# A LoRA projection bound by its DMA: first load ahead of the entry barrier, small loads on a second queue, and one chunk's casting held back until two stores have landed

## Chip, cores, metric

The kernel runs on one core of a Trainium2 chip. The metric is the device time of one execution in microseconds, lower is better. Where two kernels are compared, they ran on the same chip, in alternating rounds.

## The reference

```python
x_flat = x.reshape(-1, in_dim)             # 32768 x 256, float32
y = x_flat @ W                             # W: 256 x 256
lora_out = (x_flat @ lora_A) * lora_E      # rank 16
y = y + scale * (lora_out @ lora_B)
return y.reshape(batch, seq_len, out_dim).astype(np.float32)
```

The input x is 33.6 MB and the output is 33.6 MB. Both cross between HBM and SBUF once (the page of the kernel before: HBM read 33.85 MB, written 33.56 MB), so the kernel moves 67 MB whatever it computes.

## The kernel before

The kernel folds the LoRA part into one weight, `weff = W + A diag(E) B`, and then works on 8 chunks of 4 MB. A chunk is loaded into one of 6 "homes" in SBUF. It is treated in 8 groups: GpSimd casts a group to bf16, TensorE transposes it, ScalarE copies the transposed group out of PSUM, TensorE multiplies, and VectorE writes the result back over the input in the home. Then the home is stored. Two homes are used twice, so chunks 6 and 7 can be loaded only after chunks 0 and 1 are stored.

All DMAs are issued by SyncE (SP), in this order:

```python
ORDER = ["L0", "L1", "L2", "L3", "L4", "L5",
         "S0", "S1", "L6", "L7", "S2", "S3", "S4", "S5", "S6", "S7"]

def sync_program():
    def load(pc):
        c, s, e = pc
        if c >= N_HOMES:
            sync.wait_ge(stored_of[c - N_HOMES], 16)
        sync.dma_start(out=home(c)[:, s:e, :], in_=x_chunks[c, :, s:e, :]).then_inc(loaded[pc], 16)

    load(pieces[0])                        # first 1 MB of chunk 0
    for name, to, of in (("w", ...), ("a", ...), ("e", ...), ("b", ...)):
        sync.dma_start(out=to[:], in_=of).then_inc(set_up_loaded[name], 16)
    for step in ORDER:
        ...                                # loads as above; a store waits for its chunk:
        sync.wait_ge(s_chunk, c + 1)
        sync.dma_start(out=y_chunks[c], in_=home(c)[:]).then_inc(stored_of.get(c, stored_rest), 16)

def gpsimd_program():
    ...                                    # identity matrix for the transposes
    for g in range(N_GROUPS):              # 64 groups
        c, b = g // GPC, g % GPC * CG
        for pc in pieces:
            if pc[0] == c and pc[1] == b:
                gpsimd.wait_ge(loaded[pc], 16)
        if g >= NS:
            gpsimd.wait_ge(s_turned, g - NS + 1)
        gpsimd.tensor_copy(out=stage[g % NS][:], in_=home(c)[:, b:b + CG, :]).then_inc(s_stage, 1)
    ...

# ... (scalar_program, vector_program, tensor_program cut)
with tc.tile_critical(no_gpsimd_drain=True):
    sync_program(); gpsimd_program(); scalar_program(); vector_program(); tensor_program()

def wait_for_stores(nc):
    nc.sync.wait_ge(stored_rest, 16 * N_HOMES).then_inc(stored_rest, -16 * N_HOMES)

nc.at_finalize(wait_for_stores)
```

Of the kernel before, what the change touches and what calls it, by code (L numbers as in the profile page):

```python
# [15 lines left out]
N_HOMES = 6  # L16
# [5 lines left out]
]  # L22

EARLY_AFTER = 1

CG = 4
GPC = ROWS // CG
# [8 lines left out]
def kernel(  # L36
# [10 lines left out]
    nc = tc.nc  # L47
# [5 lines left out]
    KT = K // P  # L53
    assert N == N_CHUNKS * ROWS * P and K == M and KT == 2

    x_chunks = x_flat.rearrange("(c p b) k -> c p b k", p=P, b=ROWS)
# [8 lines left out]
    w_sb = sbuf("w_sb", [P, KT, M], FP32)  # L65
    a_sb = sbuf("a_sb", [P, KT, R], FP32)
    b_sb = sbuf("b_sb", [R, M], FP32)
    e_sb = sbuf("e_sb", [R, 1], FP32)
# [5 lines left out]
    pieces = []  # L74
    for c in range(N_CHUNKS):
        s = 0
# [3 lines left out]
    loaded = {pc: sem(f"loaded_{pc[0]}_{pc[1]}") for pc in pieces}  # L80
    set_up_loaded = {n: sem(f"loaded_{n}") for n in ("w", "a", "b", "e")}
    stored_of = {c: sem(f"stored_{c}") for c in range(N_CHUNKS - N_HOMES)}
    stored_rest = nc.alloc_semaphore("stored_rest")
# [12 lines left out]
    def home(c):  # L96
        return homes[c % N_HOMES]

    sync, gpsimd, scalar, vector, tensor = nc.sync, nc.gpsimd, nc.scalar, nc.vector, nc.tensor

    def sync_program():
        def load(pc):
            c, s, e = pc
            if c >= N_HOMES:
                sync.wait_ge(stored_of[c - N_HOMES], 16)
            sync.dma_start(out=home(c)[:, s:e, :], in_=x_chunks[c, :, s:e, :]).then_inc(loaded[pc], 16)

        load(pieces[0])
        for name, to, of in (
            ("w", w_sb, W.rearrange("(q t) m -> q t m", t=KT)),  # L110
            ("a", a_sb, lora_A.rearrange("(q t) r -> q t r", t=KT)),
            ("e", e_sb, lora_E[:, None]),
            ("b", b_sb, lora_B),
        ):
            sync.dma_start(out=to[:], in_=of).then_inc(set_up_loaded[name], 16)
        for step in ORDER:
            c = int(step[1:])
            if step[0] == "L":
                for pc in pieces:
                    if pc[0] == c and pc != pieces[0]:  # L120
                        load(pc)
                if c == EARLY_AFTER:

                    sync.wait_ge(s_first, 1)
                    sync.dma_start(out=y_chunks[0, :16, 0, :32], in_=home(0)[:16, 0, :32]).then_inc(s_early, 16)
            else:
                sync.wait_ge(s_chunk, c + 1)
                if c == 0:
                    sync.wait_ge(s_early, 16)
                sync.dma_start(out=y_chunks[c], in_=home(c)[:]).then_inc(stored_of.get(c, stored_rest), 16)  # L130

    def gpsimd_program():
        gpsimd.memset(ident[:], 0.0).then_inc(s_ident, 1)  # L133
        gpsimd.wait_ge(s_ident, 1)
        gpsimd.affine_select(  # L135
            out=ident[:],
            in_=ident[:],
            compare_op=ALU.not_equal,
            fill=1.0,
            base=0,  # L140
            pattern=[[-1, P]],
            channel_multiplier=1,
        ).then_inc(s_ident, 1)
        for g in range(N_GROUPS):
            c, b = g // GPC, g % GPC * CG
            for pc in pieces:
                if pc[0] == c and pc[1] == b:
                    gpsimd.wait_ge(loaded[pc], 16)
            if g >= NS:
                gpsimd.wait_ge(s_turned, g - NS + 1)  # L150
            gpsimd.tensor_copy(out=stage[g % NS][:], in_=home(c)[:, b:b + CG, :]).then_inc(s_stage, 1)  # L151

        gpsimd.wait_ge(s_turned, N_GROUPS - NS + 1)
        gpsimd.drain().then_inc(s_stage, 1)

    def scalar_program():
        for g in range(N_GROUPS):
            scalar.wait_ge(s_turned, g + 1)
            if g >= NX:
                scalar.wait_ge(s_y, g - NX + 1)  # L160
            halves = psum_xt[g % NT][:].bitcast(BF16).rearrange("q b (p t) -> q b t p", t=KT)
            scalar.copy(out=xt[g % NX][:], in_=halves).then_inc(s_xt, 1)  # L162

    def vector_program():
        vector.wait_ge(set_up_loaded["e"], 16)
        vector.wait_ge(s_pe_set_up, 1)
        vector.tensor_scalar(  # L167
            out=ate[:],
            in0=psum_y[0][:R, :KT, :P],
            scalar1=e_sb[:],  # L170
            scalar2=float(scale),
            op0=ALU.mult,
            op1=ALU.mult,
        ).then_inc(s_ate, 1)
        vector.wait_ge(set_up_loaded["w"], 16)
        vector.wait_ge(s_pe_set_up, 2)
        vector.tensor_add(out=weff[:], in0=w_sb[:], in1=psum_y[1][:, :KT, :]).then_inc(s_free, NY)  # L177
        for g in range(N_GROUPS):
            c, b = g // GPC, g % GPC * CG
            vector.wait_ge(s_y, g + 1)  # L180
            vector.tensor_copy(out=home(c)[:, b:b + CG, :], in_=psum_y[g % NY][:]).then_inc(s_free, 1)  # L181
            if g == 0:
                vector.drain().then_inc(s_first, 1)
            if g % GPC == GPC - 1:
                vector.drain().then_inc(s_chunk, 1)

    def tensor_program():
        def take(s):
            tensor.wait_ge(s, 1).then_inc(s, -1)  # L189

        def turn(i):
            take(s_stage)

            words = stage[i % NS][:].bitcast(FP32)
            for b in range(CG):
                ins = tensor.transpose(psum_xt[i % NT][:, b, :], words[:, b, :], ident[:])  # L196
            ins.then_inc(s_turned, 1)

        def multiply(i):
            take(s_xt)  # L200
            take(s_free)
            for b in range(CG):
                for t in range(KT):
                    ins = tensor.matmul(  # L204
                        psum_y[i % NY][:, b, :],
                        xt[i % NX][:, b, t, :],
                        weff[:, t, :],
                        start=(t == 0),
                        stop=(t == KT - 1),
                    )  # L210
            ins.then_inc(s_y, 1)

        tensor.wait_ge(s_ident, 2)
        tensor.wait_ge(set_up_loaded["a"], 16)
        for t in range(KT):
            ins = tensor.transpose(psum_y[0][:R, t, :P], a_sb[:, t, :], ident[:])  # L216
        ins.then_inc(s_pe_set_up, 1)
        turn(0)
        tensor.wait_ge(set_up_loaded["b"], 16)
        tensor.wait_ge(s_ate, 1)  # L220
        for t in range(KT):
            ins = tensor.matmul(psum_y[1][:, t, :], ate[:, t, :], b_sb[:], start=True, stop=True)  # L222
        ins.then_inc(s_pe_set_up, 1)
        assert N_GROUPS % UNROLL == 0 and all(UNROLL % n == 0 for n in (NS, NX, NT, NY))
        with tensor.Fori(0, N_GROUPS // UNROLL):
            for i in range(UNROLL):
                turn(i + 1)
                multiply(i)

    with tc.tile_critical(no_gpsimd_drain=True):  # L230
        sync_program()
        gpsimd_program()
        scalar_program()
        vector_program()
        tensor_program()

    def wait_for_stores(nc):
        nc.sync.wait_ge(stored_rest, 16 * N_HOMES).then_inc(stored_rest, -16 * N_HOMES)

    nc.at_finalize(wait_for_stores)  # L240


# [33 lines left out]
```

## Time and profile before

| | before |
|---|---|
| time, median (lowest to highest) | 163.35 us (163.25 to 163.46, 3 runs) |
| profiled span | 162.0 us |
| bytes moved, mean rate over the span | 67.43 MB, 416 GB/s |
| compute ends (last VectorE copy) | 121.2 us |
| last DMA completion | 162.0 us |

The page of the kernel before. The first lines give busy time; in the part with 40 slices each digit is the busy share of one slice, about 4 us, in tenths.

```profile
span 162.0 us, 2150 instructions
PE 96.9 (60%) x778; PEld 80.1 (49%) x778; DVE 79.6 (49%) x66; ACT 66.1 (41%) x65; POOL 67.1 (41%) x70
...
PE   0399928999999999999900089999960000000000
...
DMA  5999898999999997999999999999999999999992
...
DMA packets 2979, 67.43 MB, mean 416 GB/s; under 512 B 528, under 2 KB 544, under 8 KB 672
```

No compute engine is busy for more than 60% of the span, and TensorE is done after three quarters of it. The DMA row reads 7 to 9 tenths from the second slice to the last but one. So the kernel can get faster only where DMA time is lost, and that is at its two ends and in packets that take longer than they should. Note the three empty slices in TensorE's row: between 82 and 93 us it has nothing to do although DMA is loading.

The head, by the timeline (start, duration, engine, line, what; "SPq" is the SP queue issuing a DMA):

```profile
0.94 0.38 SPq L106 DMA_DIRECT2D home<-in_x_dram  x1
...
1.38 0.42 SPq L115 DMA_DIRECT2D w_sb<-in_W_dram  x1
...
3.59 1.37 SPq L106 DMA_DIRECT2D home<-in_x_dram  x3
```

The first load is issued at 0.94 us, and its first packet starts at 1.95. The view of SP's waits says what it waited for before that (engine and line, releaser, us in total, times, longest): 0.7 us, for TensorE at the entry barrier.

```profile
SPq L257 <- PEq L257: 0.7, 1, 0.7
```

GpSimd's casts around the idle stretch, by its timeline; the bracket is the idle time before the instruction and what ended it:

```profile
76.09 1.04 POOL L151 CAST stage<-home 128x1024 bf16<-128x1024 f32 x1 [0.38 <-PE psum_xt L196]
77.48 1.04 POOL L151 CAST stage<-home 128x1024 bf16<-128x1024 f32 x1 [0.35 <-PE psum_xt L196]
92.77 2.03 POOL L151 CAST stage<-home 128x1024 bf16<-128x1024 f32 x2 [14.24 <-DMA home<-in_x_dram]
```

The sixth chunk is cast up to 78.5 us, and then nothing can be cast until chunk 6 has been loaded. During these casts, and until 83 us, DMA is storing chunks 0 and 1. During the idle stretch it is loading.

One fact is not in these views: the duration of the single DMA packets, which the trace records. Of the 1920 packets of 32 KB, 1453 take exactly 1213 ns and most others 1214 to 1221. The trace does not say which of the 16 DMA engines moved a packet, but packets that follow each other at their own distance form a chain. I listed the 32 KB packets of 1260 to 1345 ns, called "slow packets" below. In the kernel before they are, from 62 us on:

```
start of the slow packets, us
beside stores 0 and 1, compute running:  64.6 65.9 67.2 68.5 69.7 71.0 72.3 72.4 73.6 74.9 76.2 77.5 78.7 80.0
beside loads 6 and 7 (83 to 100 us):     none
beside stores 2 and 3, compute running:  100.2 104.8 106.1 107.3 108.6 109.9 111.2 112.5 113.8 115.1 116.4 117.6 118.9 121.4 122.7
```

With few exceptions (72.4, 100.2) each starts when the one before has ended (within a row of them the starts are 1.27 to 1.32 us apart), so I take them for the packets of one engine. (The one at 72.4 follows an 8 KB packet that fetched instructions, the page's "q14 instruction", at 72.05 us. It overlaps the packet before it in the list, so I give it to another engine.) That engine falls behind. Packets longer than 1345 ns are not in the list: they stand at the turns from loads to stores (near 60 and 100 us) and beside later instruction fetches, and one of 1619 ns at 100.7 us seems to be of the same engine, so not quite all of its lag comes from slow packets. The trace has 16 completions for each large load or store, which I take for one of each engine, and the kernel's waits are for all 16. For the last store the median of the 16 completions is at 159.80 us, the second-last at 160.21 and the last at 162.00. The kernel ends when this one engine does.

### The profile page before, as it was taken

The page shows a single profiled execution, that of the slowest core. Times are in us where ns is not written, and L with a number is a line of the kernel's source. Part 1 is how long each engine was busy: PE and PEld are TensorE (multiplying, and loading weights), DVE is VectorE, ACT ScalarE, POOL GpSimd, SP SyncE. Part 2 cuts the span into 40 slices and gives each one's busy share as a digit, 9 for nine tenths or more (in the row PEclk, how much of TensorE's full clock was granted, in tenths as well). Part 3 has the DMA queues.
Part 4 walks back from the last instruction along what each step waited for, and adds up shares of the span by engine and source line. Part 5 has one row for each costly group of instructions (what it writes and reads, how often), then busy time and mean ns, then how long its engine had stood idle before and what let it go on. Part 6 is the DMA issues. An engine that isn't in the chain of part 4 may idle for free. (4 is left out here: it accounts for less than half of the span.)

```text
span 162.0 us, 2150 instructions
## 1 busy us (share of the span) xinstructions
PE 96.9 (60%) x778; PEld 80.1 (49%) x778; DVE 79.6 (49%) x66; ACT 66.1 (41%) x65; POOL 67.1 (41%) x70
## 2 busy tenths in 40 slices
PE   0399928999999999999900089999960000000000
PEld 0268817888888888888800068888840000000000
DVE  0116854888888888888830017888880000000000
ACT  3044725777767677777700026676720000000000
POOL 1455518777777677777200066677500000000000
PEclk9999999999999999999995558999995555555555
DMA  5999898999999997999999999999999999999992
GB/s 166 419 455 457 388 518 388 388 518 388 388 518 388 388 512 324 461 390 429 469 396 429 469 396 429 455 421 429 445 429 429 445 421 453 421 429 445 421 429 105
DMA packets 2979, 67.43 MB, mean 416 GB/s; under 512 B 528, under 2 KB 544, under 8 KB 672
## 3 DMA queue, kind: packets, MB, share of 16 engines
q1 hardware_dynamic: 2976, 67.41, 97.5%
q14 instruction: 3, 0.02, 0.0%
HBM read 33.85 MB, written 33.56 MB: 416 GB/s over the span
## 5 line engine op out<-in xcount | busy, mean ns | idle before, releaser
L181 DVE COPY home<-psum_y 128x1024 f32<-128x1024 f32 x64 | 78.4, 1225 | 31.9 <-PE psum_y L204 29.9
L151 POOL CAST stage<-home 128x1024 bf16<-128x1024 f32 x64 | 66.4, 1042 | 47.8 <-DMA home<-in_x_dram 26.0
L162 ACT COPY xt<-psum_xt 128x1024 bf16<-128x1024 bf16 x64 | 64.8, 1012 | 51.6 <-PE psum_xt L196 51.6
L204 PE MATMUL psum_y<-weff,xt 128*128 128x256 bf16 x512 | 68.4, 278 | 0.4
L204 PEld LDWEIGHTS psum_y<-weff,xt 128*128 128x128 bf16 x512 | 47.0, 99 | 14.4 <-issue 6.4
L196 PE MATMUL psum_xt<-ident,stage 128*128 128x128 f32 x260 | 41.1, 283 | 16.0 <-PEq L189 16.0
L196 PEld LDWEIGHTS psum_xt<-ident,stage 128*128 128x128 f32 x260 | 31.9, 147 | 18.1 <-issue 17.2
L216 PE MATMUL psum_y<-ident,a_sb 128*16 128x128 f32 x2 | 0.6, 394 | 6.6 <-DMA a_sb<-in_lora_A_dram 6.6
L167 DVE TENSOR_SCALAR ate<-psum_y,e_sb 16x256 f32<-16x256 f32 x1 | 0.5, 472 | 7.3 <-PE psum_y L216 7.3
L216 PEld LDWEIGHTS psum_y<-ident,a_sb 128*16 128x16 f32 x2 | 0.1, 90 | 6.6 <-issue 6.6
L222 PE MATMUL psum_y<-b_sb,ate 16*128 16x256 f32 x4 | 2.1, 670 | 0.0
L177 DVE TENSOR_TENSOR weff<-w_sb,psum_y 128x512 bf16<-128x512 f32 x1 | 0.7, 689 | 2.4 <-PE psum_y L222 2.4
L162 ACT ACT_TABLE_LOAD x1 | 1.3, 1283 | 0.9 <-SPq L230 0.9
L222 PEld LDWEIGHTS psum_y<-b_sb,ate 16*128 16x128 f32 x4 | 1.2, 319 | 0.5 <-issue 0.3
L133 POOL MEMSET ident<- 128x128 f32 x1 | 0.2, 206 | 0.5 <-SPq L230 0.5
L135 POOL TENSOR_SCALAR_AFFINE_SELECT ident<-ident 128x128 f32<-128x128 f32 x1 | 0.3, 293 | 0.2 <-POOL ident L133 0.2
L257 POOL MEMSET const-float32-0.0<- 128x1 f32 x1 | 0.1, 99 | 0.2 <-issue 0.2
L257 POOL MEMSET const-bfloat16-1.0<- 128x1 bf16 x1 | 0.1, 103 | 0.0
L257 POOL MEMSET const-uint8-127<- 128x1 uint8 x1 | 0.1, 103 | 0.0
L257 POOL MEMSET const-float32-1.0<- 128x1 f32 x1 | 0.1, 99 | 0.0
## 6 DMA issues: line engine op xcount, KB each, us to landing
out_dram<-home SPq DMA_DIRECT2D x8, 4096.0 KB, 43.3
home<-in_x_dram SPq DMA_DIRECT2D x7, 4096.0 KB, 19.7
home<-in_x_dram SPq DMA_DIRECT2D x2, 1024.0 KB, 5.0
home<-in_x_dram SPq DMA_DIRECT2D x1, 2048.0 KB, 9.7
w_sb<-in_W_dram SPq DMA_DIRECT2D x1, 256.0 KB, 4.9
a_sb<-in_lora_A_dram SPq DMA_DIRECT2D x1, 16.0 KB, 4.6
e_sb<-in_lora_E_dram SPq DMA_DIRECT2D x1, 0.1 KB, 4.4
b_sb<-in_lora_B_dram SPq DMA_DIRECT2D x1, 16.0 KB, 3.8
```

The source lines that it names most:

```text
L133: gpsimd.memset(ident[:], 0.0).then_inc(s_ident, 1)
L135: gpsimd.affine_select(out=ident[:], in_=ident[:], compare_op=ALU.not_equal, fill=1.0, base=0, pattern=[[-1, P]], channel_multiplier=1,).t ...
L151: gpsimd.tensor_copy(out=stage[g % NS][:], in_=home(c)[:, b:b + CG, :]).then_inc(s_stage, 1)
L162: scalar.copy(out=xt[g % NX][:], in_=halves).then_inc(s_xt, 1)
L167: vector.tensor_scalar(out=ate[:], in0=psum_y[0][:R, :KT, :P], scalar1=e_sb[:], scalar2=float(scale), op0=ALU.mult, op1=ALU.mult,).then_in ...
L177: vector.tensor_add(out=weff[:], in0=w_sb[:], in1=psum_y[1][:, :KT, :]).then_inc(s_free, NY)
L181: vector.tensor_copy(out=home(c)[:, b:b + CG, :], in_=psum_y[g % NY][:]).then_inc(s_free, 1)
L196: ins = tensor.transpose(psum_xt[i % NT][:, b, :], words[:, b, :], ident[:])
L204: ins = tensor.matmul(psum_y[i % NY][:, b, :], xt[i % NX][:, b, t, :], weff[:, t, :], start=(t == 0), stop=(t == KT - 1),)
L216: ins = tensor.transpose(psum_y[0][:R, t, :P], a_sb[:, t, :], ident[:])
L222: ins = tensor.matmul(psum_y[1][:, t, :], ate[:, t, :], b_sb[:], start=True, stop=True)
L257: nc = _bacc.Bacc("TRN2", target_bir_lowering=False, num_devices=1)
```

## The change

The intent: start the DMA earlier, take the small loads out of the way of the large ones, and move the compute of the sixth chunk out of the stretch in which chunks 0 and 1 are stored. The core of the diff:

```diff
+HELD = N_HOMES - 1
 ...
+    opening = []
+    def ahead_of_entry_barrier(nc):
+        ...  # moves each instruction named in `opening` ahead of its engine's first Drain,
+        ...  # that is, ahead of the entry barrier
+    nc.at_finalize(ahead_of_entry_barrier)
 ...
-        load(pieces[0])
-        for name, to, of in (("w", ...), ("a", ...), ("e", ...), ("b", ...)):
-            sync.dma_start(out=to[:], in_=of).then_inc(set_up_loaded[name], 16)
+        opening.append(load(pieces[0]).ins.name)
 ...
+            if (c, b) == (HELD, 0):
+                for held_by in stored_of.values():
+                    gpsimd.wait_ge(held_by, 16)
             if g >= NS:
                 gpsimd.wait_ge(s_turned, g - NS + 1)
             gpsimd.tensor_copy(...)
 ...
     def scalar_program():
+        for name, to, of in (("a", ...), ("e", ...), ("b", ...), ("w", ...)):
+            ins = scalar.dma_start(out=to[:], in_=of).then_inc(set_up_loaded[name], 16)
+            if name == "a":
+                opening.append(ins.ins.name)
 ...
+    def wait_for_stores(nc): ...      # the same function, registered
+    nc.at_finalize(wait_for_stores)   # before the engine programs
 ...
-    def wait_for_stores(nc): ...      # instead of after them
-    nc.at_finalize(wait_for_stores)
```

The last part changes nothing: in both built programs the wait for the last six stores is SP's last instruction, after the closing barriers.

More of the change, by code (lines that the diff above doesn't have):

```diff
@@ L99 @@
     sync, gpsimd, scalar, vector, tensor = nc.sync, nc.gpsimd, nc.scalar, nc.vector, nc.tensor
+    opening = []
+    def ahead_of_entry_barrier(nc):
+        blocks = nc.main_func.blocks
+        for name in opening:
+            block = next(b for b in blocks if any(i.name == name for i in b.instructions))
+            ins = next(i for i in block.instructions if i.name == name)
+            assert not ins.sync_info.on_wait
+            block.instructions = [i for i in block.instructions if i.name != name]
+            first = blocks[0].instructions
+            at = next(
+                n for n, i in enumerate(first) if i.engine == ins.engine and isinstance(i, mybir.InstDrain)
+            )
+            blocks[0].instructions = first[:at] + [ins] + first[at:]
+    nc.at_finalize(ahead_of_entry_barrier)
     def sync_program():
@@ L105, in load @@
                 sync.wait_ge(stored_of[c - N_HOMES], 16)
-            sync.dma_start(out=home(c)[:, s:e, :], in_=x_chunks[c, :, s:e, :]).then_inc(loaded[pc], 16)
-        load(pieces[0])
-        for name, to, of in (
-            ("w", w_sb, W.rearrange("(q t) m -> q t m", t=KT)),
-            ("a", a_sb, lora_A.rearrange("(q t) r -> q t r", t=KT)),
-            ("e", e_sb, lora_E[:, None]),
-            ("b", b_sb, lora_B),
-        ):
-            sync.dma_start(out=to[:], in_=of).then_inc(set_up_loaded[name], 16)
+            ins = sync.dma_start(out=home(c)[:, s:e, :], in_=x_chunks[c, :, s:e, :])
+            return ins.then_inc(loaded[pc], 16)
+        opening.append(load(pieces[0]).ins.name)
         for step in ORDER:
@@ L156, in scalar_program @@
     def scalar_program():
+        for name, to, of in (
+            ("a", a_sb, lora_A.rearrange("(q t) r -> q t r", t=KT)),
+            ("e", e_sb, lora_E[:, None]),
+            ("b", b_sb, lora_B),
+            ("w", w_sb, W.rearrange("(q t) m -> q t m", t=KT)),
+        ):
+            ins = scalar.dma_start(out=to[:], in_=of).then_inc(set_up_loaded[name], 16)
+            if name == "a":
+                opening.append(ins.ins.name)
         for g in range(N_GROUPS):
@@ L228, in tensor_program, with wait_for_stores @@
                 multiply(i)
+    def wait_for_stores(nc):
+        nc.sync.wait_ge(stored_rest, 16 * N_HOMES).then_inc(stored_rest, -16 * N_HOMES)
+    nc.at_finalize(wait_for_stores)
     with tc.tile_critical(no_gpsimd_drain=True):
@@ L235 @@
         tensor_program()
-    def wait_for_stores(nc):
-        nc.sync.wait_ge(stored_rest, 16 * N_HOMES).then_inc(stored_rest, -16 * N_HOMES)
-    nc.at_finalize(wait_for_stores)
 _INS = ['x', 'W', 'lora_A', 'lora_B', 'lora_E', 'scale']
```

## The prediction

> **What bounds the kernel.** The DMA engines. The page gives 67.43 MB at a mean 416 GB/s over a span of 162.0 us. In the DMA records a 32 KB packet takes 1213 ns, so 16 engines can move 432 GB/s; 67.43 MB then need 156.1 us (estimate from these numbers).[...] Compute ends at 121.2 us, DMA at 161.5. About 6 us are lost: about 2.6 us at the head (first load issued at 0.94 us by the timeline, first packet at 1.95, back-to-back packets only from 2.7), about 0.5 us where loads turn into stores (packets of up to 2.0 us around 60 us), and 1.8 us at the end: of the last store's 16 completions 15 are in by 160.2, the last one at 162.0. One DMA engine straggles: in the records a single chain of packets of about 1285 ns (not 1213) runs from 64.6 to 81 us and from 104.8 to 124 us, the two stretches where stores and compute overlap. While compute ran beside loads (0 to 59, 94 to 101) there is none.
>
> **What the change does.**
> 1. The first 1 MB load and the lora_A load go ahead of the entry barrier. The waits of the SP queue show SP waiting 0.7 us there; its issue should move from 0.94 to about 0.0-0.2 us. This lies wholly on the critical path: all DMA shifts about 0.85 us earlier.
> 2. W, A, E, B go to ACT's queue.[...] SP's next load is issued at about 1 us, not 3.59, but the first 1 MB covers that in both. Worth about 0.1 us.
> 3. "Late wait for stores": in the built program the wait is SP's last instruction in both kernels. Worth 0.
> 4. The hold. Casting of the sixth chunk moves from about 66 us to about 82 us, when the second store has landed. Compute of this chunk (about 14 us) leaves the store stretch and goes beside the loads of the last two chunks. At 1.41 us a group, after the slow start seen at 93-99 us, compute again ends near 121 us (estimate); the last store is not due until about 149. So it costs nothing, and the straggler is spared about 9-10 slow packets of 72 ns: about 0.7 us, on the critical path because the straggler ends last.
>
> **Prediction.** 163.35 - 0.9 - 0.7 = 161.7 us; 80% range 160.8 to 162.7. Chances: faster by over 2% 4%, within 2% 95.5%, slower by over 2% 0.5%.
>
> **What would show it.** Step 1: the first load at under 0.3 us in the timeline, first 1 MB landed near 4.6 us (before 5.5). Step 2: a DMA row without a dip in the first 8 us after it starts. Step 4: POOL idle from about 67 to 82 us, released by the store; no idle stretch at 82-92; slow packets gone from about 70-81; last completion about 1.1 us after the others instead of 1.8.
>
> **What would make it wrong.** The slow packets may follow compute itself, and move with the compute to 82-102: then only 0.9 us. Or the lag vanishes wholly (down to about 160.7). The early load may delay the barrier and give less than 0.9.

The forecast's sum is 163.35 less 0.9 for the early load and 0.7 for the hold, 161.7 us. The 0.1 us of step 2 is the author's estimate and has no term of its own in the sum.

## The result, and the profile after

| | before | after |
|---|---|---|
| time, median (lowest to highest) | 163.36 us (163.25 to 163.46, 4 runs) | 161.91 us (161.83 to 162.12, 4 runs) |
| profiled span | 162.0 us | 160.5 us |
| mean DMA rate over the span | 416 GB/s | 420 GB/s |
| compute ends | 121.2 us | 123.1 us |
| last store: median, second-last, last of 16 completions | 159.80, 160.21, 162.00 us | 158.82, 160.43, 160.47 us |

The ratio is 0.9914, with a 95% interval of 0.9896 to 0.9931. A ratio here is the mean time of one kernel's runs over that of the other's runs of the same rounds, so it is not quite the ratio of the medians quoted. The change is worth 1.45 us, or 0.9%, well clear of noise and below the 2% at which a difference is called faster.

The page after:

```profile
span 160.5 us, 2151 instructions
PE 98.3 (61%) x778; PEld 81.1 (51%) x778; DVE 79.6 (50%) x66; ACT 66.1 (41%) x65; POOL 67.1 (42%) x70
...
PE   0565999999999999940009999999993000000000
...
DMA  7999999999999999999999999999999999999993
...
DMA packets 2979, 67.43 MB, mean 420 GB/s; under 512 B 528, under 2 KB 544, under 8 KB 672
```

TensorE's empty slices have moved from about 82-93 us to about 70-83, and the first slice of the DMA row has gone from 5 to 7. The busy time of the large copies is unchanged: no engine's work became cheaper.

The head after, by the timeline:

```profile
0.00 2.44 SPq L127 DMA_DIRECT2D home<-in_x_dram  x4
0.12 0.38 ACTq L181 DMA_DIRECT2D a_sb<-in_lora_A_dram  x1
...
1.99 0.48 ACTq L181 DMA_DIRECT2D w_sb<-in_W_dram  x1
```

The first load is now the first thing in the span, and the same view of SP's waits shows a shorter wait at the barrier, 0.3 us and not 0.7. Issuing the load seems to have filled the rest (it took 0.38 us in the kernel before):

```profile
SPq L284 <- PEq L284: 0.3, 1, 0.3
```

The first packet starts at 1.01 us instead of 1.95. The median completion of the last store comes 0.98 us earlier (159.80 to 158.82), so the whole shift of the head arrives at the end.

GpSimd's casts around the idle stretch after the change:

```profile
65.06 1.04 POOL L169 CAST stage<-home 128x1024 bf16<-128x1024 f32 x1 [0.27 <-PE psum_xt L223]
66.57 1.04 POOL L169 CAST stage<-home 128x1024 bf16<-128x1024 f32 x1 [0.47 <-PE psum_xt L223]
82.81 2.03 POOL L169 CAST stage<-home 128x1024 bf16<-128x1024 f32 x2 [15.21 <-DMA out_dram<-home]
```

The wait is as long as before, but it lies beside the stores, and it ends with a store instead of a load. The slow packets after the change:

```
start of the slow packets, us
beside stores 0 and 1:             63.7 65.0 66.2 67.5 68.8          (none from 72 to 83)
beside loads 6 and 7 (83 to 98):   none
beside stores 2 and 3:             100.4 101.7 103.0 104.3 105.6 106.8 108.1 109.4 110.7 112.0
                                   113.3 114.6 115.8 117.1 118.4 119.7 121.0 123.5 124.8
```

Two other things moved that need an explanation. W lands later, although it is issued only 0.6 us later (1.99 and not 1.38 us). These are the page's lines of DMA issues (KB each, us from issue to landing), first before, then after:

```profile
w_sb<-in_W_dram SPq DMA_DIRECT2D x1, 256.0 KB, 4.9
```

```profile
w_sb<-in_W_dram ACTq DMA_DIRECT2D x1, 256.0 KB, 10.9
```

And in the last store the second-last engine is now nearly as late as the last one.

### The profile page after: what moved, and what is told of

Read it like the earlier page. It is cut to its first block, busy times and chain, and to the rows that moved or that the text cites. A ratio compares the mean times of both kernels' runs of the same rounds, so it can differ in the third digit from the quotient of the medians.

```text
span 160.5 us, 2151 instructions
## 1 busy us (share of the span) xinstructions
PE 98.3 (61%) x778; PEld 81.1 (51%) x778; DVE 79.6 (50%) x66; ACT 66.1 (41%) x65; POOL 67.1 (42%) x70
## 5 line engine op out<-in xcount | busy, mean ns | idle before, releaser
L208 DVE COPY home<-psum_y 128x1024 f32<-128x1024 f32 x64 | 78.4, 1226 | 31.0 <-PE psum_y L231 28.2
L231 PE MATMUL psum_y<-weff,xt 128*128 128x256 bf16 x512 | 69.5, 281 | 4.1 <-PEq L216 3.3
L231 PEld LDWEIGHTS psum_y<-weff,xt 128*128 128x128 bf16 x512 | 47.6, 100 | 18.1 <-issue 10.4
L223 PE MATMUL psum_xt<-ident,stage 128*128 128x128 f32 x260 | 41.6, 285 | 14.1 <-PEq L216 14.1
## 6 DMA issues: line engine op xcount, KB each, us to landing
w_sb<-in_W_dram ACTq DMA_DIRECT2D x1, 256.0 KB, 10.9
```

The source lines that it names most:

```text
L208: vector.tensor_copy(out=home(c)[:, b:b + CG, :], in_=psum_y[g % NY][:]).then_inc(s_free, 1)
L223: ins = tensor.transpose(psum_xt[i % NT][:, b, :], words[:, b, :], ident[:])
L231: ins = tensor.matmul(psum_y[i % NY][:, b, :], xt[i % NX][:, b, t, :], weff[:, t, :], start=(t == 0), stop=(t == KT - 1),)
```

## Experiments

Three chips were used: the first four experiments ran on one, the next three on the second, the last two on the third. The kernel before had medians of 163.37, 163.50 and 163.67 us on them, so experiments of different chips are compared by their ratio to it. The first four take the change apart: with the kernels before and after they give six of the eight combinations of early load, second queue and hold.

### Early first load alone

```diff
 # the changed kernel, but
-    scalar: loads of a, e, b, w;  a also ahead of the barrier
+    sync, behind the early first load: loads of w, a, e, b
-            if (c, b) == (HELD, 0): ...
```

> Early first load alone: the four small loads stay on SP's queue, no hold. Theory: all DMA shifts by the 0.94 us by which the first load is issued earlier; the slow packets stay as in the kernel before, and the last completion stays about 2.2 us behind the median of the last store's 16 completions. Time 162.4 us. Rival (the early load gains little by itself, it is the other queue for the small loads that fills the head): over 162.9 us.

Measured: 162.45 us, ratio 0.9944 (0.9926 to 0.9962). The median completion of the last store is at 158.81 us, 0.99 earlier than before, and the last one is 1.97 us behind it. The slow packets are all there, 8 and 7 beside the first two stores. The early load is worth about 0.9 us and does not need the second queue.

### Hold alone

```diff
 # the kernel before, and in gpsimd_program
+            if (c, b) == (N_HOMES - 1, 0):
+                for held_by in stored_of.values():
+                    gpsimd.wait_ge(held_by, 16)
```

> The hold alone, on the kernel before. Theory: the packets of about 1285 ns vanish from about 70 to 81 us (about 9 of them), the straggling engine ends about 0.65 us earlier, the rest as before. Time 162.7 us. Rival (slow packets follow compute wherever it goes): as many packets of 1285 ns as before, now between 82 and 100 us, time 163.4 us.

Measured: 162.80 us, ratio 0.9958 (0.9941 to 0.9975), that is 0.57 us by the medians. The median completion of the last store has not moved at all (159.80 us in both), but the last comes 1.70 us behind it and not 2.20. One slow packet is left from 72 to 83 us, where there were 8; none appeared from 83 to 98 us, where the compute went. The rival falls: slow packets do not follow compute, they need stores beside it.

### The change without its hold

```diff
 # the changed kernel, but
-            if (c, b) == (HELD, 0):
-                for held_by in stored_of.values():
-                    gpsimd.wait_ge(held_by, 16)
```

> The changed kernel without its hold. Theory: slow packets again from 64 to 80 us; the straggling engine, which ended equal to a second late engine in the changed kernel, ends about 0.65 us later, alone: 162.5 us. If the late engine from the head is the one that also collects the slow packets here, more: 163.0 us. Rival (the hold is worth nothing, the head is all): 161.9 us.

Measured: 162.33 us, ratio 0.9963. The interval, 0.9918 to 1.0007, is wide because one of the six runs took 164.65 us; the other five lie between 162.30 and 162.51. The median says that the hold's absence costs 0.42 us against the 161.91 of the changed kernel, which was timed in another session, whose chip the record does not name, with the same time for the kernel before (163.36 and 163.37). Eight slow packets are back between 72 and 83 us (one of them, as in the kernel before, beside an instruction fetch at 72.1 us). This is less than the 0.65 us expected.

### Early load and hold, small loads on the first queue

```diff
 # the changed kernel, but
-    scalar: loads of a, e, b, w;  a also ahead of the barrier
+    sync, behind the early first load: loads of w, a, e, b
```

> The changed kernel with the four small loads back on SP's queue, behind the early first load. In the changed kernel two engines complete the second 1 MB load about 1 us after the median of the 16, in the kernel before 0.13 us. Theory: the second queue makes this spread; without it the spread at that load is about 0.2 us, all engines are 0.95 us ahead of the kernel before by the second chunk, and the time depends on the slow-packet engine alone: 161.7 us, 0.2 below the changed kernel. Rival (the other queue helps by 0.1 to 0.3 us as it lets the second load start sooner): 162.1 us.

Measured: 161.85 us, ratio 0.9906 (0.9889 to 0.9924). The changed kernel has 161.91 and 0.9914. So the second queue is worth nothing that these runs can tell. The spread of the second 1 MB load (last completion behind the median) is 0.16 us here and 1.06 us in the changed kernel, as expected; but this had no price, because the slow-packet engine ends about 1.6 us behind the median in either kernel.

This run also gives a better figure for the hold: against "early first load alone", on the same chip and in the same rounds, it is 0.60 us faster (162.45 and 161.85), and the intervals of the two ratios do not touch.

The second queue does explain W. With one queue, in this run, W lands 4.4 us after its issue (4.9 in the kernel before), with the second queue 10.9. In the changed kernel W's 128 packets of 2 KB start between 5.85 and 11.78 us, among 167 packets of x of 8 or 16 KB (most 309, or 611 to 620 ns); in the kernel before, where they stand in one queue with x, all 128 start between 4.94 and 5.75, and with them only 6 packets of x. The first result is written by VectorE at 15.7 us and not 12.9. A 2 KB store of this result waits for it, and behind that store SP's loads of chunks 2 to 5, issued from 17.44 us and not 14.62. Chunk 1 was being loaded until 22.6 us (median of its completions), so the queue did not run dry (DMA share 0.98 from 12 to 17 us, 1.08 from 17 to 22.6).

### What in the compute makes a packet slow: number of instructions or volume of data?

The next three kernels add work after the last chunk, beside stores only, where the changed kernel has none. The work changes no output. The first adds very many, very small instructions on VectorE.

```diff
 # the changed kernel, at the end of vector_program
+        for n in range(400):
+            vector.memset(w_sb[:, n // M, n % M:n % M + 1], 0.0)
```

> What in the compute slows one DMA engine beside stores? The changed kernel, and after its last chunk VectorE does 400 memsets of one column each[...], beside stores only. Theory N (the number of instructions): packets of about 1285 ns go on to about 150 us, some 15 to 20 more; the slow engine ends 1 to 1.4 us later, 163.1 us. Theory V (the volume of data that the engines move through SBUF): no slow packet after 126 us, 161.9 us.

Measured: 163.42 us, ratio 1.0006 (0.9986 to 1.0027); the changed kernel has 0.9914. The text above lets the memsets last to about 150 us. That was the estimate. In this run 128 of them took 3.63 us, 28 ns each, and they were over by 137 us. By the windows view (length of the window, then busy time and, in brackets, the instructions of each engine; the last three columns are TensorE's clock, the DMA share and GB/s):

```profile
126.00:136.00 10.00, 0.00 (x0) 0.00 (x0) 6.76 (x240) 0.00 (x0) 0.00 (x0) 0.50 1.01 431
```

Slow packets ran on to 132.6 us, with two more at 136.3 and 137.7. So 24 instructions a microsecond with next to no data (128x1 f32 each) slow the engine. This run has a flaw as a test of time: its 400 instructions had to be fetched, in three 8 KB packets at 128.6, 134.2 and 139.8 us, and next to each a 32 KB packet took 1650 to 1695 ns. Part of the 1.5 us is theirs: judged by the completions of one store after another, an engine falls behind by about 0.8 us at each fetch and ends last, 2.65 us behind the median, while the slow-packet engine ends 2.32 us behind (about 1.6 in the changed kernel).

The second adds few, large instructions on three engines.

```diff
 # the changed kernel, at the end of vector_program, gpsimd_program, scalar_program
 # (each after waits for all compute to be done)
+        for _ in range(23): vector.drain(); vector.tensor_copy(out=psum_y[0][:], in_=home(4)[:, :CG, :])
+        for _ in range(27): gpsimd.drain(); gpsimd.tensor_copy(out=stage[0][:], in_=home(4)[:, :CG, :])
+        for _ in range(27): scalar.drain(); scalar.copy(out=xt[0][:], in_=halves)
```

> The changed kernel, and after its last chunk VectorE, ScalarE and GpSimd go on with some 25 of their large copies each (1.2, 1.0, 1.0 us; about 3 instructions a us with full data volume) while TensorE rests, from 123 to about 152 us, beside stores only. Theory V: slow packets go on to about 152 us, some 20 more, 163.3 us. Theory N: few or none after 126 us, 161.9 us.

Measured: 162.27 us, ratio 0.9941 (0.9914 to 0.9968). The three engines were busy all the time, as in the main loop, with 2.7 instructions a microsecond:

```profile
126.00:150.00 24.00, 0.00 (x0) 0.00 (x0) 22.59 (x20) 22.63 (x23) 21.39 (x21) 0.50 0.99 427
```

From 126 to 154 us there is not one packet of 1260 ns or more. Instead 15 packets took 1226 to 1246 ns, which is 13 to 33 ns too long. The two slow packets after that, at 154.1 and 156.1 us, start when the copies have ended (153.8), the second beside an instruction fetch at 155.8. (The drains between the copies are not counted as instructions in this view; they would at most double the rate.) So the result is neither of the two extremes: full data volume with few instructions gives a small slowing.

The third adds TensorE alone.

```diff
 # the changed kernel, at the end of tensor_program
+        for _ in range(NY): take(s_free)
+        with tensor.Fori(0, 8):
+            for i in range(4):
+                ...  # the 8 matmuls of multiply(i), without its waits
```

> The changed kernel, and after its last multiplication TensorE alone does another 32 groups of 8 matmuls with their 8 weight loads (about 0.9 us a group at the full clock, 18 instructions a us; no DMA and no other engine has part in it), from 123 to about 151 us. Theory N: slow packets go on to about 151 us, some 20 more, 163.3 us. Theory V:[...] few or none, 161.9 us.

Measured: 163.19 us, ratio 0.9979 (0.9962 to 0.9995). It is a loop, but one 16 KB packet of instructions was fetched at 126.9 us, and a 32 KB packet took 1612 ns beside it. That was another engine's, which ended about 1.1 us behind the median; the slow-packet engine ended last, 2.76 us behind.

```profile
126.00:150.00 24.00, 24.00 (x223) 21.51 (x221) 0.00 (x0) 0.00 (x0) 0.00 (x0) 1.00 1.00 429
```

The slow packets run on without a break of more than one or two packets to 151.5 us, 19 of them after 126 us, and stop where TensorE stops. With two of a little under 1260 ns they add 1.28 us to their engine, and the time rises by 0.65% of 163.5, about 1.1 us. TensorE alone, with 18.5 instructions a microsecond (223 and 221 in 24 us) and none of the other engines' copies, does what the whole main loop does (18.4: 164, 162, 15, 14 and 12 instructions between 62 and 82 us of the kernel before). What the volume theory would give here was the author's assumption about how much TensorE reads, which no run shows; so it is the other two runs that speak against the volume.

The three together: 2.7 instructions a microsecond cost 13 to 33 ns in a packet. About 18 cost 63 ns in a slow packet on the mean with matmuls alone and about 75 ns in the main loop of the kernel before; 24 a microsecond cost 95 ns with memsets of one column. The volume of data does not order the memsets and the large copies; the number of instructions nearly orders all of these runs. Semaphores are not the cause: neither the memsets nor the added matmuls signal one (the trace of the changed kernel has 1238 semaphore updates, these two have 1238 and 1236). Nor is TensorE's granted clock, 0.50 beside the memsets and 1.00 beside the matmuls.

### Hold released by the first store

```diff
-                for held_by in stored_of.values():
-                    gpsimd.wait_ge(held_by, 16)
+                gpsimd.wait_ge(stored_of[0], 16)
```

> The hold is released by the first store alone (about 73 us, not 82.6). Theory (each us of compute taken out of the first two stores spares slow packets there): about half the hold's gain, 3 to 5 slow packets come back between 74 and 82 us, and compute ends earlier by a few us, so that one to three drop out at 121 us: 162.1 us, between 161.9 and 162.33. Rival (only a hold to the end of the second store helps, or any hold does): 162.33 or 161.9.

Measured: 162.17 us, ratio 0.9906 (0.9887 to 0.9925), beside 163.67 for the kernel before on this chip. In the trace 4 slow packets are back from 72 to 83 us, one of them beside an instruction fetch at 80.9 us (none in the changed kernel, 8 before). In time this cannot be told from the changed kernel: the difference to be seen is about 0.2 us and the interval is 0.6 us wide. The profiled execution was also an unusual one of 164.35 us, with a stretch around 22 to 30 us in which packets of all engines took up to 2.3 us. The engine that ended last there had been 2.3 us behind since that stretch; the slow-packet engine ended 1.42 us behind. The packet count supports the theory; the time is inconclusive.

### Hold kept until the last load

```diff
-                for held_by in stored_of.values():
-                    gpsimd.wait_ge(held_by, 16)
+                gpsimd.wait_ge(loaded[pieces[-1]], 16)
```

> The hold is kept until the last load has landed (about 102 us): all compute of the last three chunks then runs beside stores, 102 to about 141 us, and the last stores are still issued in time (the seventh chunk done near 128, the last near 141, due by about 139 and 149). Theory (it is compute beside stores that costs, not early compute): about 8 slow packets at 63 to 71 and about 30 from 102 to 143 us, 38 in all against about 23: 162.9 us, the hold's gain lost though the wait is longer. Rival (the hold helps because it spares the first two stores): 161.9 us.

Measured: 163.06 us, ratio 0.9972 (0.9946 to 0.9999). Only 0.6 us of the change's 1.45 are left by the medians, less than the early load alone gives. From 72 to 83 us there is no slow packet, as in the changed kernel, but they now run from 109.1 to 145.0 us, 14 of them after 126. So it is not the sparing of the first two stores that pays; it pays to put compute beside loads. In the profiled execution the slow-packet engine ends 2.54 us behind the median of the last store, while another engine, which lost time in the head and at the two turns from loads to stores, ends 2.86 us behind. So this run's time is not the slow packets' alone.

### All runs

| kernel | ratio to before | slow packets 62-72 us | 72-83 | 83-98 | 100-126 | 126-157 | last store: last completion behind the median, us |
|---|---|---|---|---|---|---|---|
| before | 1 | 6 | 8 | 0 | 15 | 0 | 2.20 |
| after | 0.9914 | 5 | 0 | 0 | 19 | 0 | 1.65 |
| early load alone | 0.9944 | 8 | 7 | 0 | 14 | 0 | 1.97 |
| hold alone | 0.9958 | 7 | 1 | 0 | 16 | 0 | 1.70 |
| without the hold | 0.9963 | 8 | 8 | 0 | 14 | 0 | 2.19 |
| early load, hold, one queue | 0.9906 | 5 | 0 | 0 | 17 | 0 | 1.65 |
| tiny instructions added | 1.0006 | 5 | 0 | 0 | 17 | 8 | 2.65 |
| large copies added | 0.9941 | 4 | 0 | 0 | 16 | 2 | 1.84 |
| matmuls added | 0.9979 | 5 | 0 | 0 | 20 | 19 | 2.76 |
| hold to the first store | 0.9906 | 6 | 4 | 0 | 17 | 0 | 2.42 |
| hold to the last load | 0.9972 | 5 | 0 | 0 | 15 | 14 | 2.86 |

The table leaves out 98 to 100 us, the second turn from loads to stores, where one to five packets of 1260 to 1345 ns stand in five of the runs. The last column is not always the slow-packet engine's: in "tiny instructions added", "hold to the first store" and "hold to the last load" that engine ends 2.32, 1.42 and 2.54 us behind.

No version clearly beats the changed kernel. The one without the second queue equals it and is simpler.

## Why the prediction was right

The prediction said 161.7 us in 160.8 to 162.7; the measured time is 161.91.

1. *Early load: 0.9 us, wholly on the critical path.* Right. The first load moved from 0.94 to 0.00 us, its first packet from 1.95 to 1.01. By itself it gave 0.92 us (163.37 to 162.45). The first 1 MB landed at 4.74 us (predicted 4.6, before 5.57).
2. *Second queue: about 0.1 us.* Right that it hardly matters; the 0.1 us was the author's estimate. Measured: nothing (161.85 without it, 161.91 with it). The prediction did not see that it would unbalance the engines. In the changed kernel's profiled execution two engines were 0.7 and 0.9 us behind the median already after the first chunk (at most 0.15 before). In six of the seven profiled executions with the second queue the last engine was 0.84 to 1.11 us behind there (0.16 in the seventh), in the four without it at most 0.23.
3. *Late wait: 0.* Argued from the built program. No run tests it alone, as the program would be the same.
4. *Hold: 0.7 us.* The mechanism was right, the size too large: 0.57 us on the kernel before, 0.60 us beside the early load, 0.42 us in the changed kernel. The term that was mis-sized is "compute again ends near 121 us": it ended at 123.1. (The kernel before needed 28.4 us for its last 16 groups, from 92.77 us. Eight groups more at 1.41 us each, from 82.81, would have given about 122.5, an estimate from its own trace.) From 62 to 83 us the hold spared nine slow packets, as forecast: 5 are left, and what they took over 1213 ns adds up to 0.35 us; the kernel before has 14, and 1.04 us. But stores 2 and 3 then had 19 slow packets and not 15, worth 1.48 us and not 1.17, because compute ended later while the stores came earlier. So 0.32 of the 0.69 us were given back; the same sum against the kernel without the hold leaves 0.48 us, beside 0.42 measured. A smaller miss: the last completion was forecast 1.1 us after the others, and one other engine was equally late, held up in the head by the second queue and at the turns from loads to stores.

Why does the hold cost so little? GpSimd waits for about 15 us in either kernel (14.24 and 15.21), and TensorE with it. Before, it was idle while chunk 6 was being loaded, the kind of stretch in which compute did no harm here (no slow packet from 83 to 98 us in any run), and busy while chunks 0 and 1 were stored. The hold only exchanges the two. It also shows the limit: 90 us of compute (64 groups at 1.41 us) do not fit beside 78 us of loads (8 at 9.7 us each; both are estimates from distances in the trace), the first of which has nothing to compute yet, so some compute must run beside stores.

What stays open: why instructions slow one DMA engine's stores. No run here shows it. An explanation would have to fit three findings: only stores suffer (no slow packet from 83 to 98 us in any run), the number of instructions counts and not the volume of data (63 to 95 ns on the mean at 18 to 24 a microsecond, 13 to 33 ns at 2.7), and the slow packets go on for a packet or two after the compute has ended (124.8 us against 123.1). Every run was recorded with its span and clock, so none can tell whether an execution that is not recorded has them too, and with them the hold's gain.

Also open is the turn from loads to stores. From 57 to 61.5 us, where the first store follows the sixth load, 22 packets of 32 KB took over 1345 ns in the kernel before (the longest 2032) and 23 in the changed kernel (the longest 1738); at the second such turn, from 98 to 103 us, 3 and 2 did. (Instructions were fetched at 59.4 and 102.3 us in the kernel before, at 57.3 us in the changed one.) No experiment here explains it.

## What to carry to other kernels

When DMA is full from end to end, look at the first packet, at the last completion, and at the single packets in between. Here an average of 416 GB/s hid that one of 16 completions of the last store came 2.20 us behind the median, and the kernel ended with it. If compute has slack, where it runs can still matter, so choose what it runs beside; here an idle stretch of 15 us cost nothing beside stores, and was wasted beside loads (the hold was worth 0.42 to 0.60 us). A first load that depends on nothing did not have to wait at the entry barrier here: issued at 0.00 us and not 0.94, it gave 0.92 us by itself.
